# The gate of the down stage summed row by row in VectorE, its neighbour sum by accumulating DMAs, and values back in a new order

## The chip, the cores and the metric

The kernel runs on one core of a Trainium2 chip. The time is that of one execution on the device, in microseconds (us). Five engines matter: TensorE (PE, its weight loads PEld), VectorE (DVE), ScalarE (ACT), GpSimd (POOL) and SyncE (SP). Each takes its instructions in order and waits on semaphores for the others. SP, POOL and ACT also issue DMAs.

## The reference

One transformer block over 512 tokens of width 2048. An adaptive layer norm makes six rows of 2048 numbers from the condition `c`; attention and a short convolution stand in the middle; the part that matters here is the feed-forward end, with 5632 columns:

```python
sh_a, sc_a, g_a, sh_f, sc_f, g_f = jnp.split(jax.nn.silu(c) @ ada_w[l] + ada_b[l], 6, axis=-1)
...
x = x + g_a[:, None, :] * (jnp.concatenate([y_conv, y_attn], axis=-1) @ w_out[l])

h = modulate(rms_norm(x, norm_ffn[l]), sh_f, sc_f)
x = x + g_f[:, None, :] * ((jax.nn.silu(h @ ffn_w1[l]) * (h @ ffn_w3[l])) @ ffn_w2[l])
```

All is float32. `g_f`, the last sixth, is the gate of the down stage: silu(c) times 2048 rows of `ada_w`.

## The kernel before

Every weight is split into a high and a low half (`whi`, rounded by a cast in ACT, L905; `wlo`, the rest, by a subtraction in DVE, L910), so that products of halves give float32 accuracy. The order of the instructions on each engine is set by a scheduler that keeps to the order of the code where it can.

The last stages are these. **w_out** (to 895 us) multiplies the mixed values by `w_out`, adds them to x (L856 and after) and prepares the second norm. The **up stage** (917 to 1862 us) goes over 44 blocks u of 128 columns of `ffn_w1` and `ffn_w3`. For each, `blocks` loads four pieces of 512 KB on SP's queue (11 and 21, the upper and lower half of the rows of w1; 12 and 22, of w3), 128 partitions with eight pieces of 512 bytes each. The first two blocks (`PLAIN`) are multiplied plainly. Every later one takes a Strassen-like scheme of seven products in place of eight, with sums of the weight pieces:

- `sum5`: t = 11 + 12 into a tile of the pool `t2`; `sum6`: t += 22; `sum7`: 12 += 22; `sum4`: 21 += t. All four are DVE instructions of 128x1024, at L1006.
- The products p1, p5, p6, p3, p2, p7 and p4 multiply piece 11, t after sum5, t after sum6, 22, 21, the sum in 12 and the sum in 21 by the prepared inner values `hC[p]`. Each product is 16 matmuls (L917 with whi, L919 with wlo) into one of the PSUM banks x, y and z; p4 of a block is done two products into the next block (`late`).
- `post` evicts: ACT copies half a bank (L927), DVE adds the other (L928) or adds both (L924), ACT applies Silu, DVE multiplies (L1040), and `store` writes the 128 columns to the DRAM tensor `gd` on POOL's queue (L969).

A step of the main loop prepares the sums three products ahead (five for p4), the splits two ahead, and then issues its matmuls and its eviction. Raw pieces stand in `ring[0]` (4 buffers) and, for two blocks of three, in `raw2` (8 buffers, opened at step 7, when the memory of the second norm is free).

Beside this runs `gate_rows`, a generator of which the loop takes a step every third product. It computes `g_f` in four pieces of 512 columns. For each of 16 rows k of a piece it loads 128x512 of `ada_w` into the one buffer `raw` (L1107, 256 KB, POOL's queue), scales it in ACT by silu(c) (L1108) and adds it to `acc` in POOL (L1109). Both tiles are called `acc` in the profile and in the rows below. A matmul with ones sums over partitions, and a DMA keeps the result in `gfd`.

The **down stage** (1875 to 2281 us) multiplies by `ffn_w2` in the same manner, groups b of ten blocks. `k_load` reads five blocks of `gd` per half (L1164, POOL's queue), `a_parts` splits them (ghi in ACT at L1196, glo in DVE at L1197), `w_load` loads weights on SP and adds a second piece by an accumulating DMA of POOL's queue (L1208). `multiply` is L1248. A **tail** does the last four blocks and writes out 512 columns at a time.

## Time and profile before

| | us |
|---|---|
| median of 3 runs | 2335.28 |
| lowest, highest | 2333.3, 2337.05 |
| the profiled execution | 2334.18 |
| its span in the trace | 2332.4 |
| mean granted TensorE clock | 0.981 |

The span runs from the first to the last recorded instruction; 1.8 us of the execution lie around it. In a row of a group, the words behind the line and the engine are the operation, what it writes and reads by the program's names, the size in partitions x elements, and a count; in brackets at the end of a row of the timeline stands the idle time of the engine before the instruction and what ended it. In the rows of one source line three durations in ns follow (least, median, largest) and the first and last start. A row of the waits names the engine, tile and line that waited, whom it waited for, and the total, the times and the longest.

### The profile page before, as it was taken

The page shows a single profiled execution, that of the slowest core. Times are in us where ns is not written, and L with a number is a line of the kernel's source. Part 1 is how long each engine was busy: PE and PEld are TensorE (multiplying, and loading weights), DVE is VectorE, ACT ScalarE, POOL GpSimd, SP SyncE. Part 2 cuts the span into 40 slices and gives each one's busy share as a digit, 9 for nine tenths or more (in the row PEclk, how much of TensorE's full clock was granted, in tenths as well). Part 3 has the DMA queues.
Part 4 walks back from the last instruction along what each step waited for, and adds up shares of the span by engine and source line. Part 5 has one row for each costly group of instructions (what it writes and reads, how often), then busy time and mean ns, then how long its engine had stood idle before and what let it go on. Part 6 is the DMA issues. An engine that isn't in the chain of part 4 may idle for free. (4 is left out here: it accounts for less than half of the span.)

```text
span 2332.4 us, 30434 instructions
## 1 busy us (share of the span) xinstructions
PE 2205.1 (95%) x11401; PEld 1829.1 (78%) x11401; DVE 1795.3 (77%) x2555; ACT 1028.1 (44%) x1618; POOL 291.2 (12%) x381
## 2 busy tenths in 40 slices
PE   6999999999999997999989889899999889999998
PEld 5788788787787785788878778788888767787877
DVE  6868478878757745888778788788888767788888
ACT  5335245555542225444444444444444454444441
POOL 5400000000000012200320312300000021111001
PEclk9999999999999998999999999999999989999999
DMA  9964555544346853544444444444443388676645
GB/s 323 364 208 138 168 173 172 150 137 141 107 134 238 301 193 95 170 129 122 141 131 122 142 130 139 133 122 122 122 122 105 115 256 259 173 243 188 173 136 171
DMA packets 344928, 391.14 MB, mean 168 GB/s; under 512 B 16788, under 2 KB 257656, under 8 KB 343628
## 3 DMA queue, kind: packets, MB, share of 16 engines
q1 hardware_dynamic: 314556, 281.36, 38.3%
q0 software_dynamic: 30224, 107.84, 15.7%
q8 instruction: 89, 1.46, 0.2%
q14 instruction: 59, 0.48, 0.1%
HBM read 369.21 MB, written 19.93 MB: 167 GB/s over the span
## 5 line engine op out<-in xcount | busy, mean ns | idle before, releaser
L917 PE MATMUL main<-hC,whi 128*128 128x512 f32 x1408 | 369.7, 406 | 41.0 <-DVE d L924 21.2
L910 DVE TENSOR_TENSOR wlo<-raw,whi 128x1024 fp32r<-128x1024 f32 x218 | 270.5, 1241 | 113.5 <-ACT whi L905 112.9
L905 ACT CAST whi<-raw 128x1024 fp32r<-128x1024 f32 x238 | 248.7, 1045 | 210.5 <-PE main L917 99.3
L917 PEld LDWEIGHTS main<-hC,whi 128*128 128x128 f32 x1408 | 261.4, 195 | 95.9 <-DVE d L928 19.2
L917 PE MATMUL aux<-hC,whi 128*128 128x512 f32 x1072 | 272.1, 396 | 5.7 <-ACT whi L905 5.2
L905 ACT CAST whi<-t 128x1024 fp32r<-128x1024 f32 x144 | 151.1, 1051 | 194.1 <-PE aux L917 47.7
L917 PEld LDWEIGHTS aux<-hC,whi 128*128 128x128 f32 x1072 | 194.7, 191 | 43.7 <-ACT whi L905 6.7
L919 PEld LDWEIGHTS main<-hC,wlo 128*128 128x128 f32 x1408 | 195.8, 194 | 15.7 <-DVE wlo L910 1.4
L919 PE MATMUL main<-hC,wlo 128*128 128x256 f32 x1408 | 200.0, 286 | 0.0
L92 ACT CAST whi<-raw 128x1024 fp32r<-128x1024 f32 (+2 forms) x92 | 87.9, 958 | 214.3 <-PE main L100 137.0
L98 PE MATMUL main<-alo,whi 128*128 128x512 f32 x448 | 180.1, 402 | 1.4 <-DVE alo L346 1.4
L185 DVE SCALAR_TENSOR_TENSOR acc<-araw,cT,acc 128x512 f32<-128x512 f32 x184 | 137.8, 750 | 55.8 <-DMA araw<-in_ada_w 48.6
L99 PE MATMUL main<-ahi,wlo 128*128 128x512 f32 x448 | 176.8, 395 | 0.0
L100 PE MATMUL main<-ahi,whi 128*128 128x512 f32 x448 | 176.5, 394 | 0.0
L919 PEld LDWEIGHTS aux<-hC,wlo 128*128 128x128 f32 x1072 | 146.8, 191 | 12.7 <-DVE wlo L910 2.4
L93 DVE TENSOR_TENSOR wlo<-raw,whi 128x1024 fp32r<-128x1024 f32 (+2 forms) x92 | 102.0, 1113 | 68.1 <-ACT whi L92 67.3
L98 PE MATMUL main<-wlo,ahi 128*128 128x512 f32 x384 | 152.5, 397 | 1.1 <-DVE t L856 0.9
L919 PE MATMUL aux<-hC,wlo 128*128 128x256 f32 x1072 | 151.0, 284 | 0.8 <-DVE wlo L910 0.8
L99 PE MATMUL main<-whi,alo 128*128 128x512 f32 x384 | 150.4, 392 | 0.0
L100 PE MATMUL main<-whi,ahi 128*128 128x512 f32 x384 | 150.3, 391 | 0.0
L1248 PE MATMUL main<-wlo,ghi 128*128 128x512 f32 x280 | 110.7, 397 | 21.0 <-ACT ghi L1196 13.3
L910 DVE TENSOR_TENSOR wlo<-t,whi 128x1024 fp32r<-128x1024 f32 x84 | 104.4, 1243 | 25.3 <-ACT whi L905 25.3
(332 smaller groups left out, 4337.3 us busy)
## 6 DMA issues: line engine op xcount, KB each, us to landing
raw<-in_ffn_w SPq DMA_DIRECT2D x204, 512.0 KB, 4.0
w<-in_ffn_w SPq DMA_DIRECT2D x60, 512.0 KB, 5.9
araw<-in_ada_w POOLq DMA_DIRECT2D x56, 512.0 KB, 14.4
araw<-in_ada_w SPq DMA_DIRECT2D x112, 256.0 KB, 2.9
raw<-in_w_in SPq DMA_DIRECT2D x128, 192.0 KB, 2.7
araw<-in_ada_w SPq DMA_DIRECT2D x40, 512.0 KB, 5.5
raw<-in_w_in SPq DMA_DIRECT2D x37, 512.0 KB, 5.3
raw<-in_w_out SPq DMA_DIRECT2D x32, 512.0 KB, 5.8
```

Source lines behind the costliest of these rows:

```text
L92: nc.scalar.copy(hi[:, :m], raw[:, :m])
L93: nc.vector.tensor_sub(lo[:, :m], raw[:, :m], hi[:, :m].bitcast(F32))
L98: nc.tensor.matmul(ps, lhs[0], rhs[1], start=first, stop=False)
L99: nc.tensor.matmul(ps, lhs[1], rhs[0], start=False, stop=False)
L100: nc.tensor.matmul(ps, lhs[0], rhs[0], start=False, stop=last)
L185: nc.vector.scalar_tensor_tensor(acc, w, s, acc, op0=ALU.mult, op1=ALU.add)
L905: nc.scalar.copy(hi, t)
L910: nc.vector.tensor_sub(lo, t, hi.bitcast(F32))
L917: nc.tensor.matmul(ps, wt[0][:, ks[k]], hC[p][:, k, :], start=first and k == 0, stop=False, skip_group_check=True)
L919: nc.tensor.matmul(ps[:, HS:], wt[1][:, ks[k]], hC[p][:, k, 0:HS], start=False, stop=last and k == HK - 1, skip_group_check=True)
L1248: nc.tensor.matmul(ps[2 * t + c], x_[:, j, tok], w[:, cs], start=m == 0 and j == 0 and p in (1, 5, 2), stop=m == 2 and j == GC - 1 and p i ...
```

## The change

In `gate_rows` the ACT scale and the POOL add become one DVE instruction (raw times silu(c) plus acc), and the generator's `yield` stands between the DMA and this instruction. `sum5` is gone: from block 2 on, `blocks` loads piece 11 twice, the second time into the tile t, and POOL's queue issues an accumulating DMA that adds piece 12 to it. Odd blocks go to `raw2` and fill five of its buffers, even ones to `ring[0]` and `t2`. The pools `up` and `t2` stay open through the down stage. The tiles hC are allocated in another order; the last block's products come as p1, p5, p4 of the block before, p6, p3, p7, p2, p4. The post of the very last product is put behind the first `a_parts` of the down stage, and its store goes on ACT's queue. In the down stage the first splits of weights come ahead of the first `a_parts`, the calls of `a_parts` for p1 and p5 of a group and `k_load` come at other products, and the tail takes its columns in the order 2, 3, 0, 1.

```diff
--- before.py
+++ after.py
@@ -883,10 +883,10 @@
 
     HS, HK = S // 2, KC // 2
     ust = ExitStack()
+    dp = pool("up", 2)
+    t2p = pool("t2", 1)
     hcp = pool("hC", 1, stack=ust)
-    hC = {p: hcp.tile([P, HK, S], F32R, name=f"hC{p}") for p in (1, 2, 5, 6, 3, 7, 4)}
-    dp = pool("up", 2, stack=ust)
-    t2p = pool("t2", 1, stack=ust)
+    hC = {p: hcp.tile([P, HK, S], F32R, name=f"hC{p}") for p in (1, 5, 6, 3, 7, 2, 4)}
     PLAIN = 2
     NU = FF // P
     zone = {0: ring[0]}
@@ -894,10 +894,15 @@
     def blocks(u):
 
         b = {}
-        pl = zone[1] if u > PLAIN and u % 3 else ring[0]
-        for q, w, r0 in ((11, w1, 0), (21, w1, HK), (12, w3, 0), (22, w3, HK)):
-            b[q] = pl.tile([P, HK * P], F32, tag="raw", name="raw")
-            nc.sync.dma_start(b[q].rearrange("p (k n) -> p k n", k=HK), rows(w, r0, HK, u * P, P))
+        pl = zone[1] if u % 2 and 1 in zone else ring[0]
+        src = {q: rows(w, r0, HK, u * P, P) for q, w, r0 in ((11, w1, 0), (21, w1, HK), (12, w3, 0), (22, w3, HK))}
+        for name in (11, 21, 12, 22) if u < PLAIN else (11, "t", 21, 12, 22):
+            pl_, tag = (t2p, "t2") if name == "t" and pl is ring[0] else (pl, "raw")
+            b[name] = pl_.tile([P, HK * P], F32, tag=tag, name=tag)
+            to = b[name].rearrange("p (k n) -> p k n", k=HK)
+            nc.sync.dma_start(to, src[11 if name == "t" else name])
+        if u >= PLAIN:
+            nc.gpsimd.dma_start(b["t"].rearrange("p (k n) -> p k n", k=HK), src[12], accum_op=ALU.add)
         return b
 
     def w_hi(t):
@@ -966,7 +971,7 @@
             zone[1] = pool("raw2", 8, stack=ust, side="right")
 
     def store(f, g):
-        nc.gpsimd.dma_start(gd[f], g)
+        (nc.gpsimd if f + 1 < NU else nc.scalar).dma_start(gd[f], g)
 
     def plain_steps(u):
         o = {}
@@ -1004,10 +1009,6 @@
 
         def add(to, x, y):
             nc.vector.tensor_add(to, x, y)
-
-        def sum5():
-            o["b"]["t"] = t2p.tile([P, HK * P], F32, tag="t2", name="t2")
-            add(o["b"]["t"], o["b"][11], o["b"][12])
 
         def sum6():
             add(o["b"]["t"], o["b"]["t"], o["b"][22])
@@ -1051,12 +1052,17 @@
 
         none = lambda: None
         return [make(1, 11, none, "x", True, False),
-                make(5, "t", sum5, "y", True, False),
+                make(5, "t", none, "y", True, False),
                 make(6, "t", sum6, "x", False, False),
                 make(3, 22, none, "y", False, True),
                 make(2, 21, none, "z", True, True),
                 make(7, 12, sum7, "x", False, False),
                 make(4, 21, sum4, "x", False, True)]
+
+    def last_steps(new):
+
+        p1, p5, p6, p3, p2, p7, p4 = new
+        return [p1, p5], [p6, p3, p7, p2, p4]
 
 
     order, late = [], None
@@ -1070,10 +1076,11 @@
             late = None
         if u < PLAIN:
             order += new[2:]
+        elif u == NU - 1:
+            order += last_steps(new)[1]
         else:
             order += new[2:-1]
             late = new[-1]
-    order.append(late)
 
     begun = set()
 
@@ -1105,16 +1112,15 @@
             nc.gpsimd.dma_start(acc[0:1, :], a["ada_b"][:, c0:c0 + 512])
             for k in range(KC):
                 nc.gpsimd.dma_start(raw, ada_v[:, k, c0:c0 + 512])
-                nc.scalar.activation(raw, raw, AF.Identity, scale=cT[:, k:k + 1])
-                nc.gpsimd.tensor_add(acc, acc, raw)
                 yield
+                nc.vector.scalar_tensor_tensor(acc, raw, cT[:, k:k + 1], acc, op0=ALU.mult, op1=ALU.add)
             ps = aux()
             nc.tensor.matmul(ps[0:1, :], ones[:, 0:1], acc, start=True, stop=True)
             nc.scalar.copy(raw[0:1, :], ps[0:1, :])
             nc.gpsimd.dma_start(gfd[:, n * 512:(n + 1) * 512], raw[0:1, :])
 
     gate = gate_rows()
-    lead = {id(t): 5 if t["p"] == 4 and t is not order[-1] else 3 for t in order}
+    lead = {id(t): 3 if t["p"] != 4 else 2 if t is order[-1] else 5 for t in order}
     for n in range(3):
         prepare(n, "sum")
     for n in range(2):
@@ -1123,7 +1129,7 @@
     modulated(0, 2, 2, 3)
     modulated(0, 4, 4, 3)
     for n, s in enumerate(order):
-        for m in range(n + 5, n + 2, -1):
+        for m in range(n + 5, n + 1, -1):
             if m < len(order) and lead[id(order[m])] == m - n:
                 prepare(m, "sum")
         if n + 5 < len(order):
@@ -1134,7 +1140,8 @@
         if n >= 4 * PLAIN and n % 3 == 0:
             next(gate, None)
         s["mm"](s)
-        s["post"](s)
+        if n + 1 < len(order):
+            s["post"](s)
     ust.close()
 
 
@@ -1193,8 +1200,8 @@
                 src = {5: e, 6: e, 3: e, 7: a21, 2: a12, 4: a22}[p]
         hi = gpp.tile([P, GC, HS], F32R, tag="ghi", name="ghi")
         lo = gpp.tile([P, GC, HS], F32R, tag="glo", name="glo")
-        nc.scalar.copy(hi[:, :n], src)
-        nc.vector.tensor_sub(lo[:, :n], src, hi[:, :n].bitcast(F32))
+        A_["first"] = nc.scalar.copy(hi[:, :n], src).ins
+        A_["last"] = nc.vector.tensor_sub(lo[:, :n], src, hi[:, :n].bitcast(F32)).ins
         A_[b, p] = hi, lo
 
     def w_load(b, p, j):
@@ -1272,20 +1279,28 @@
     k_load(0, 1)
     for n in range(-10, 0):
         loads(n)
-    a_parts(*prods[0])
-    for m in range(3):
-        w_sum(*units[m])
     for m in range(2):
         w_split(*units[m])
+    a_parts(*prods[0])
+    with tc.issue_after(A_["last"]), tc.issue_after(A_["first"]):
+        order[-1]["post"](order[-1])
     a_parts(*prods[1])
     nc.sync.dma_start(gf, gfd.to_broadcast([P, D]))
     for n, (b, p, j) in enumerate(units):
         if j == 0:
-            a_parts(*prods[n // GC + 2])
-            if p == 3:
+            q = n // GC
+            if p == 1 and b:
+                a_parts(b, 5)
+            if p not in (2, 4):
+                a_parts(*prods[q + 2])
+            elif p == 2:
                 k_load(b + 1, 0)
-            elif p == 2 and b + 1 < NG:
-                k_load(b + 1, 1)
+            else:
+                if b + 1 < NG:
+                    k_load(b + 1, 1)
+                a_parts(*prods[q + 1])
+                if b + 1 == NG:
+                    a_parts(*prods[q + 2])
         loads(n)
         if n + 3 < len(units):
             w_sum(*units[n + 3])
@@ -1295,7 +1310,7 @@
         if j == GC - 1:
             evict(b, p)
 
-    for n in range(4):
+    for m, n in enumerate((2, 3, 0, 1)):
         cs = slice(n * 512, (n + 1) * 512)
         for i in range(NT):
             y = y2[:, i, cs]
@@ -1303,7 +1318,7 @@
             nc.gpsimd.dma_start(r, xd[n][:, i, :])
             nc.vector.tensor_mul(y, y, gf[:, cs])
             (nc.vector.tensor_add if n < 2 else nc.vector.tensor_sub)(y, r, y)
-        pst = [(aux if n % 2 else main)() for _ in range(NT)]
+        pst = [(aux if m % 2 else main)() for _ in range(NT)]
         ws = [load_split(ring, rows(w2, f, 2, n * 512, 512), 2, 512) for f in tail[::2]]
         for i in range(NT):
             tok = slice(i % 2 * P, (i % 2 + 1) * P)
```

How this moves instructions is shown at three places. First DVE within the up stage while gate rows run, at block 10; `d_...` are the tiles of the evictions, `t_...` the third sum. Before:

```order
L928 TENSOR_TENSOR d_9879<-main,d_9879 128x256
L910 TENSOR_TENSOR wlo<-raw,whi 128x1024
L1006 TENSOR_TENSOR t_9964<-raw 128x1024
L924 TENSOR_TENSOR d_9879<-aux,d_9879 128x256
L910 TENSOR_TENSOR wlo<-raw,whi 128x1024
L924 TENSOR_TENSOR d_9879<-aux,d_9879 128x256
L1006 TENSOR_TENSOR raw<-raw 128x1024
L924 TENSOR_TENSOR d_9855<-aux,d_9855 128x256
L910 TENSOR_TENSOR wlo<-t_9964,whi 128x1024
L924 TENSOR_TENSOR d_9855<-aux,d_9855 128x256
L1006 TENSOR_TENSOR t_9964<-t_9964,raw 128x1024
L924 TENSOR_TENSOR d_9879<-main,d_9879 128x256
```

And now, in the same block:

```order
L915 TENSOR_TENSOR wlo<-raw,whi 128x1024
L933 TENSOR_TENSOR d_9868<-aux,d_9868 128x256
L1116 SCALAR_TENSOR_TENSOR acc<-acc,cT 128x512
L915 TENSOR_TENSOR wlo<-raw,whi 128x1024
L933 TENSOR_TENSOR d_9655<-main,d_9655 128x256
L1011 TENSOR_TENSOR raw<-raw,t_9692 128x1024
L1041 SCALAR_TENSOR_TENSOR d_9687<-d_9687,d_9655 128x512
L933 TENSOR_TENSOR d_9868<-main,d_9868 128x256
L915 TENSOR_TENSOR wlo<-raw,whi 128x1024
L1116 SCALAR_TENSOR_TENSOR acc<-acc,cT 128x512
L929 TENSOR_TENSOR d_9868<-aux,d_9868 128x256
L915 TENSOR_TENSOR wlo<-raw,whi 128x1024
```

The write of t from two raw pieces is no longer there, and the gate's multiply-add (L1116) stands between splits and evictions.

ACT at the same block before, with the gate's scale between the casts and the evictions:

```order
L1027 ACTIVATE d_9855<-d_9855 128x256
L1108 ACTIVATE acc<-acc,cT 128x512
L905 CAST whi<-t_9964 128x1024
L927 COPY d_10037<-main 128x256
L905 CAST whi<-raw 128x1024
L1108 ACTIVATE acc<-acc,cT 128x512
L927 COPY d_10061<-aux 128x256
L905 CAST whi<-raw 128x1024
L927 COPY d_9855<-main 128x256
L1108 ACTIVATE acc<-acc,cT 128x512
L1039 ACTIVATE d_9855<-d_9855 128x256
```

And now, where the scale is gone and only casts, evictions and Silu are left:

```order
L910 CAST whi<-raw 128x1024
L932 COPY d_9868<-main 128x256
L910 CAST whi<-raw 128x1024 x3
L1028 ACTIVATE d_9844<-d_9844 128x256
L910 CAST whi<-raw 128x1024
L932 COPY d_10025<-main 128x256
L910 CAST whi<-raw 128x1024
L932 COPY d_10049<-aux 128x256
L910 CAST whi<-raw 128x1024
L932 COPY d_9844<-main 128x256
```

Second, POOL at blocks 8 to 10. Before, each gate DMA is followed by its add:

```order
L1109 TENSOR_TENSOR acc<-acc 128x512
L1107 DMA acc<-in_ada_w 128x512
L969 DMA gd_6507<-d_9879 128x512
L1109 TENSOR_TENSOR acc<-acc 128x512
L1107 DMA acc<-in_ada_w 128x512
L1109 TENSOR_TENSOR acc<-acc 128x512
L1107 DMA acc<-in_ada_w 128x512
```

Now (L905 is the accumulating DMA, L974 the store of a block):

```order
L974 DMA gd_6506<-d_9687 128x512
L1114 DMA acc<-in_ada_w 128x512
L905 DMA t_10054<-in_ffn_w 128x8x128
L1114 DMA acc<-in_ada_w 128x512 x2
L974 DMA gd_6507<-d_9868 128x512
L1114 DMA acc<-in_ada_w 128x512
L905 DMA raw<-in_ffn_w 128x8x128
```

The adds are gone, and accumulating DMAs stand among the gate's DMAs and the stores.

Third, POOL at the end of the up stage, with the last stores to `gd` (the last block's is gd_6540) and the first reads k of the down stage. Before:

```order
L969 DMA gd_6539<-d_15662 128x512
L1303 DMA r<-xd_6493 128x512 x2
L1164 DMA k_16002<-gd_6497 128x512
L1164 DMA k_16002<-gd_6498 128x512
L1164 DMA k_16002<-gd_6499 128x512
L1164 DMA k_16002<-gd_6500 128x512
L969 DMA gd_6540<-d_15838 128x512
L1164 DMA k_16002<-gd_6501 128x512
L1164 DMA k_16008<-gd_6502 128x512
```

Now:

```order
L974 DMA gd_6539<-d_15639 128x512
L1318 DMA r<-xd_6495 128x512 x2
L1171 DMA k_15973<-gd_6497 128x512
L1171 DMA k_15973<-gd_6498 128x512
L1171 DMA k_15973<-gd_6499 128x512
L1171 DMA k_15973<-gd_6500 128x512
L1171 DMA k_15973<-gd_6501 128x512
L1171 DMA k_15979<-gd_6502 128x512
L1171 DMA k_15979<-gd_6503 128x512
```

The store of the last block is no longer on this queue, and the reads of both halves of the first group follow each other.

## The prediction

> **What bounds the kernel now.** I read the page's busy times first, then windows over the up stage (917 to 1862 us), then that stage's waits, then the timeline inside one of its slow stretches.
>
> ```profile
> PE 2205.1 (95%) x11401; PEld 1829.1 (78%) x11401; DVE 1795.3 (77%) x2555; ACT 1028.1 (44%) x1618; POOL 291.2 (12%) x381
> 960.00:1040.00 80.00, 73.14 (x396) 63.07 (x395) 63.50 (x80) 34.06 (x49) 5.70 (x6) 0.96 0.55 158
> 1120.00:1520.00 400.00, 364.81 (x1965) 312.32 (x1964) 316.70 (x383) 188.29 (x278) 106.81 (x119) 0.96 0.45 135
> 1520.00:1600.00 80.00, 80.00 (x451) 69.45 (x450) 69.07 (x93) 36.92 (x53) 2.70 (x5) 0.99 0.41 123
> 1600.00:1840.00 240.00, 240.00 (x1376) 211.22 (x1375) 205.71 (x271) 111.38 (x160) 6.47 (x12) 1.00 0.36 110
> ```
>
> PE is the bound overall. A window row gives the stretch, its length, then busy time and instruction count of PE, PEld, DVE, ACT and POOL, granted clock, DMA share and GB/s. The last row holds no gate work (POOL 6.47 us): PE never idles and does 1376/240 = 5.73 matmuls a us at clock 1.00, with DVE busy 206/240 = 86%. The 400 us row holds gate rows (POOL 106.81): 1965 matmuls, which at 5.73 need 342.7 us. So 57.3 us are lost there; by the same division 10.9 us in 960 to 1040 and 1.3 us in 1520 to 1600, **69.5 us** in all.
>
> The waits of 1120 to 1520 and the timeline at 1305 us show how:
>
> ```profile
> POOL acc L1109 <- ACT acc L1108: 143.1, 45, 4.6
> ACT acc L1108 <- DMA acc<-in_ada_w: 110.9, 42, 5.1
> DVE wlo L910 <- ACT whi L905: 58.5, 42, 3.8
> PE main L917 <- DVE d L924: 19.2, 8, 3.3
> PE main L917 <- DVE d L928: 15.5, 11, 3.2
> 1283.36 1.82 DVE L1006 TENSOR_TENSOR t<-raw 128x1024 f32<-128x1024 f32 x1
> 1286.91 1.21 DVE L1006 TENSOR_TENSOR raw<-raw 128x1024 f32<-128x1024 f32 x1
> 1305.65 0.72 ACT L1108 ACTIVATE acc<-acc,cT 128x512 f32<-128x512 f32 x1 [4.15 <-DMA acc<-in_ada_w]
> 1307.52 0.36 ACT L927 COPY d<-main 128x256 f32<-128x256 f32 x1
> 1309.80 2.50 PE L917 MATMUL main<-hC,whi 128*128 128x512 f32 x5 [3.15 <-DVE d L928]
> ```
>
> ACT is only 44% busy, but takes its instructions in order. The row's scaling (L1108) stands in that queue until its DMA lands, 111/42 = 2.6 us a time; the eviction L927 and the casts L905 stand behind it, DVE waits for the casts, and PE waits for the eviction because its bank is not free. POOL's adds are a second, smaller harm: L1006 took 1.82 us beside one and 1.21 without.
>
> **The change, part by part.**
>
> *Gate rows.* Sixty-four times an ACT scale and a POOL add go, and a DVE multiply-add comes. The trace has each, and the new one's twin at L185, with the same shape:
>
> ```profile
> L1108 ACT ACTIVATE acc<-acc,cT x64: 716/724/730, 858.5 to 1513.4; 128x512 f32<-128x512 f32 x64
> L1109 POOL TENSOR_TENSOR acc<-acc x64: 1255/1287/2970, 859.3 to 1514.2; 128x512 f32<-128x512 f32 x64
> L1107 POOL DMA_DIRECT2D acc<-in_ada_w x64: 546/553/582, 853.4 to 1510.7; - x64
> DMA to landing us min/median/max: 2.7/3.0/5.1
> L185 DVE SCALAR_TENSOR_TENSOR acc<-araw,cT,acc x184: 735/752/754, 298.2 to 834.4; 128x512 f32<-128x512 f32 x184
> L1006 DVE TENSOR_TENSOR t<-raw x42: 1208/1220/2325, 961.1 to 1830.0; 128x1024 f32<-128x1024 f32 x42
> ```
>
> DVE gets 64 x 0.752 = 48.1 us and loses the third sums, 42 x 1.22 = 51.2 us, so in total it is no busier. While the gate runs it is: a block of 128 columns takes 19.5 us (112 matmuls at 5.73), DVE now works 0.86 x 19.5 = 16.7 us in it, less 1.22, plus about 2.5 gate rows (the new DVE order) x 0.752 = 1.9, so 17.4 us or 89%. PE ran without a gap at 86%, so this should nearly hide. What is new is that the in-order wait for the row's DMA now stands on DVE. The next DMA goes out behind the multiply-add (one buffer): about 0.3 us of semaphore, then 3.0 us (5.1 at worst) to landing, 3.3 in all. Between two gate rows DVE has some 5 us of other work or more (in the piece of its new order shown above, six instructions: three of 1.2, one of 0.7 and two of 0.4 us). So a row has mostly landed. I charge 4 us of PE time for the late ones; the bounds are 0 and, if DVE waited as ACT did (2.6 us for each of the 54 rows in the up stage), all that the gate costs now. I take the near end, since the median of 3.0 is the nearest row.
>
> *First Strassen blocks.* Of the 10.9 us in 960 to 1040, the larger part is no gate loss:
>
> ```profile
> 980.00:1000.00 20.00, 15.45 (x71) 12.99 (x70) 11.35 (x15) 5.30 (x9) 0.00 (x0) 0.83 0.89 252
> 990.83 1.23 DVE L1006 TENSOR_TENSOR t<-raw 128x1024 f32<-128x1024 f32 x1 [7.02 <-DMA raw<-in_ffn_w]
> ```
>
> 71 matmuls instead of 20 x 5.73 = 115 is 7.6 us, and DVE waits there for a load of block 3, which shares the four buffers of block 2. After, block 3 is odd and loads all its five pieces into the second pool as soon as that opens. I take 6 of the 7.6 back (bounds 0 and 7.6; the loads of three blocks still collide there).
>
> *Accumulating DMAs.* 42 of them replace the sums. They are not in the up stage's trace, but the down stage has forty of the same 512 KB, in long pieces:
>
> ```profile
> L1208 POOL DMA_DIRECT2D t<-in_ffn_w x20: 848/857/941, 1871.5 to 2185.0; - x20
> DMA to landing us min/median/max: 5.1/8.8/21.2
> q1 hardware_dynamic: 50566, 25.49, 36.2%
> q1 hardware_dynamic: 10364, 35.85, 37.7%
> q0 software_dynamic: 5751, 20.20, 35.3%
> t<-in_ffn_w POOLq DMA_DIRECT2D x15, 512.0 KB, 9.5
> k<-gd POOLq DMA_DIRECT2D x25, 256.0 KB, 4.1
> w<-in_ffn_w POOLq DMA_DIRECT2D x11, 512.0 KB, 8.2
> ```
>
> The first two rows are of the whole run; the first q1 row (packets, MB, share of 16 engines) is of 1560 to 1800 us, the rest of 1940 to 2200. Up stage: 36.2% of 240 us for 25.49 MB is 1.79 us of all 16 engines for 512 KB, which go in 512-byte pieces (27.5 ns a packet on its engine). Down stage: a plain 512 KB costs 0.377 x 260 x 0.524/35.85 = 1.43 us; of q0's 0.353 x 260 = 91.8 us, 25 reads of 256 KB at that price take 17.9, which leaves 73.9/26 = 2.84 us for an accumulate, **twice a plain load**. So I take 3.6 us in the up stage, an estimate from these rows. With store and gate row (0.5 and at most 1.9 us, sized by their bytes and the two plain prices) a block then needs 5 x 1.79 + 3.6 + 2.4 = 15 of its 19.5 us: it hides. Bounds: 1.8 us (a plain load), and, if the price went by packet and not by byte, 13 us; that end is the slower rival. Issuing them costs POOL 42 x 0.86 = 36 us, where 64 x 1.29 of adds go.
>
> The Trainium skill, "DMA: Bandwidth & Descriptors", section "Why small descriptors are slow (HBM only)", puts the penalty of small pieces at about three bus cycles and 32 bytes each, which would make 512-byte pieces a fifth or so dearer by the byte. The trace agrees for plain loads (1.79 against 1.43 us); no run here shows it for accumulates. By it the sum would not change.
>
> *Ramp from w_out.* DVE's first L910 waits behind ACT's scales:
>
> ```profile
> 898.76 1.46 DVE L910 TENSOR_TENSOR wlo<-raw,whi 128x1024 fp32r<-128x1024 f32 x1 [9.18 <-ACT whi L905]
> ```
>
> With them gone the w_out residual starts earlier: 1.5 us (0 to 3).
>
> *Hand-over to the down stage.*
>
> ```profile
> 1850.14 2.12 POOL L1164 DMA_DIRECT2D k<-gd  x4
> 1857.87 2.55 PE L917 MATMUL main<-hC,whi 128*128 128x512 f32 x8 [2.08 <-DVE d L924]
> 1865.24 0.54 POOL L969 DMA_DIRECT2D gd<-d  x1 [12.98 <-DVE d L1040]
> 1868.87 2.64 POOL L1164 DMA_DIRECT2D k<-gd  x5 [2.56 <-issue]
> 1874.09 1.26 ACT L1196 CAST ghi<-k 128x1280 fp32r<-128x1280 f32 x1 [9.87 <-DMA k<-gd]
> 1875.40 1.65 PE L1248 MATMUL main<-wlo,ghi 128*128 128x512 f32 x3 [13.28 <-ACT ghi L1196]
> 1875.40:1895.00 19.60, 19.36 (x74) 15.16 (x75) 14.17 (x11) 9.22 (x11) 1.71 (x2) 0.89 1.05 308
> 1895.00:2281.00 386.00, 371.32 (x1609) 303.13 (x1608) 320.82 (x322) 178.59 (x174) 49.89 (x71) 0.99 0.66 193
> ```
>
> PE waits 2.08 us before its last product (same bank as the one before) and 13.28 us after it, because the fifth gate-and-up read (k) stands behind the last store, which waits 12.98 us for the last post. After, the store is on ACT's queue, all five reads go out near 1853 to 1856, land by 1860 (median 4.1 us in the down stage's DMA row), the cast ends near 1861. PE then waits about 2.5 us for it and runs some 2 us slow. The gap before was 2.1 + 13.3 us, and some 3.8 of low clock (the last product took 1.3 us more than its like, and 74 matmuls after the restart 19.6 us where 1609/371.32 = 4.33 a us gives 17.1): 19 us. I take 12 of it back; bounds 6 (if the first accumulates, now issued behind ten reads, come late) and 16.
>
> *Down stage and tail.* PE idles 14.7 of 386 us (last row). The reads and parts are moved by a product or two, but the waits for accumulates stay. I take 0.5 us, bounds -4 and +5.
>
> **Sum:** gate 61.9 - 4 = 58, first blocks 6, ramp 1.5, hand-over 12, rest 0.5: 78 us off the profiled run's 2334.18 gives 2256.2. The median shown is 1.1 us above that run, so **2257 us**.
>
> **Rivals.**
>
> That ACT keeps the rows is ruled out by the order above. What is left:
>
> *B: DVE becomes the gate's victim.* It is in order, and wlo and evictions stand behind a multiply-add whose row isn't there. It decides once a row lands later than some 4.7 us after its issue (5 less the semaphore). For it: the landing's maximum of 5.1, and five loads a block on the same engines. Against: the median 3.0, and 11% spare on DVE. If half of the gate's cost stays, 2257 + 58/2 + a few = about **2290**.
>
> *C, slower: accumulates of 512-byte pieces bound the up stage.* If the extra is per packet, as large as in the down stage's 4 KB pieces (1.41 us x 16/128 = 176 ns on an engine), one takes 64 x (27.5 + 176) = 13 us, and a block on average 9 + 13 + 1.5 = 23.5 against 19.5: 42 x 4 = 168 us on top of the forecast, about **2425**. It begins to bind above 9 us for one accumulate and eats the whole gain above 11. For: no row shows accumulates of small pieces. Against: plain loads in pieces eight times shorter cost only 1.79/1.43 = 1.25 times as much by the byte.
>
> *D: accumulates land late for p5 though there is room.* In even blocks about 20 us lie between issue and use (seven products of 2.8 us); beyond that PE waits. Landing was 8.8 at the median, 21.2 at most. Late by 3 us in 21 even blocks takes 63 us back: about **2320**; by 4, no gain.
>
> The skill, "SBUF — State Buffer", section "Who interferes with whom", says that POOL can be starved of the port for writing descriptors by some DVE operations, though not by tensor_tensor, and advises other queues. By that rule an 89% busy DVE would push D. Here L1107's issue stays between 546 and 582 ns among DVE's work, so this trace shows no such starving; the sum by the rule would be D's.
>
> **How the numbers follow.** Forecast 0.68 (own range 2242 to 2272), B 0.15, C 0.10, D 0.07. The range from 2242 to 2300 holds most of the first two. Faster by over 0.2% (what a measurement of this kernel can tell from no change): 0.68 + 0.15 + 0.04 of D = 0.87; within: 0.02 of D; slower: C and 0.01 of D, 0.11.
>
> **What would show it.** Right: windows of 80 us in 1120 to 1520 near 455 matmuls, DVE near 90% busy in gate phases, few waits of DVE for in_ada_w, the restart of the down stage some 3 us after the last up product. B: DVE waits for in_ada_w of 1 us and more each, and PE behind wlo. C: DMA share near 1 through the up stage. D: PE waiting before p5 of even blocks alone. The forecast fails most easily in the accumulate's price, which is carried over from long pieces to short ones.

## The result and the profile after

| | before | changed |
|---|---|---|
| median of 4 runs, us | 2334.29 | 2300.27 |
| lowest, highest | 2331.09, 2337.05 | 2297.38, 2305.64 |
| span of the profiled execution | 2332.4 | 2295.6 |

The ratio is 0.9857, with a 95% interval from 0.9835 to 0.9880: 34 us or 1.4% faster. The forecast was 2257 us, 77 us faster, with a range up to 2300. The direction came out, the size didn't: less than half of the gain is there, and the time lies just outside the range.

Where the two traces part, by stage (first and last matmul of each stage, in us):

| | before | changed | difference |
|---|---|---|---|
| start to the last product of w_out | 895.1 | 901.9 | +6.8 |
| to the first product of the up stage | 22.4 | 18.5 | -3.9 |
| up stage | 944.6 | 902.7 | -41.9 |
| to the first product of the down stage | 13.3 | 7.2 | -6.1 |
| down stage | 405.1 | 413.1 | +8.0 |
| tail | 51.9 | 52.2 | +0.3 |

The first row isn't the change's: 6 us of it arise between 740 and 820 us (312 matmuls against 339), where all engines have the same order in both kernels, and a second trace of the kernel before, below, has 905.1 there. So the 36.8 us between the traces are 42 in the up stage and 4 in the ramp, less the 7 of the first row and the 2 by which the down stage gives back more than the hand-over's 6.

The busy line of the changed kernel's page:

```profile
PE 2197.4 (96%) x11401; PEld 1822.9 (79%) x11401; DVE 1758.1 (77%) x2577; ACT 989.5 (43%) x1554; POOL 263.9 (11%) x358
```

PE has 8 us less of busy time and 37 us less of span, DVE 37 us less work, POOL 27. Its windows, with the columns of those before:

```profile
960.00:1040.00 80.00, 74.27 (x407) 64.63 (x406) 57.82 (x77) 33.06 (x46) 10.09 (x9) 0.96 0.90 211
1120.00:1520.00 400.00, 386.97 (x2174) 335.21 (x2173) 329.95 (x453) 176.32 (x255) 70.37 (x92) 1.00 0.77 196
1600.00:1760.00 160.00, 160.00 (x917) 140.74 (x916) 128.15 (x172) 73.49 (x105) 18.72 (x17) 1.00 0.73 176
```

The last row has accumulations but no gate rows, and loses no matmul. The 400 us with gate rows now have 2174 matmuls in place of 1965: at 5.73 a us they lose 20.6 us where they lost 57.3. The 80 us from 960 lose 9.0 us where they lost 10.9. The DMA share is 0.77 where it was 0.45. DVE's waits for DMAs in the 400 us (total, times, longest):

```profile
DVE raw L1011 <- DMA raw<-in_ffn_w: 31.8, 8, 5.2
DVE acc L1116 <- DMA acc<-in_ada_w: 27.3, 11, 6.5
```

The rows of three source lines, L1116, L1114 (the gate rows' DMA, its landing) and L905 (the accumulation, issue and landing):

```profile
L1116 DVE SCALAR_TENSOR_TENSOR acc<-acc,cT x64: 735/746/755, 865.1 to 1511.3; 128x512 f32<-128x512 f32 x64
DMA to landing us min/median/max: 2.6/4.2/8.6
L905 POOL DMA_DIRECT2D t<-in_ffn_w x21: 1545/1577/1618, 909.6 to 1757.6; - x21
DMA to landing us min/median/max: 6.2/8.3/11.6
```

The gate's instruction costs the 0.75 us that were expected. Gate rows land in 4.2 us, in 3.0 before. ACT's wait for rows is gone, but DVE now stands 59 us before two kinds of DMA: the seventh product's sum of even blocks (L1011) for its load, and the gate's instruction for its row. The evictions stand behind both. Of PE's 14 gaps of over 0.15 us in the 400 (12.9 us together), 12 (11.4 us) come when the sum's wait was the last that DVE had, as at 1204 us below. The gate instruction's waits take up the time that DVE has to spare before that; how much of PE's loss this makes is not shown here.

```profile
1204.04 1.23 DVE L1011 TENSOR_TENSOR raw<-raw 128x1024 f32<-128x1024 f32 x1 [5.24 <-DMA raw<-in_ffn_w]
1205.18 0.42 DVE L933 TENSOR_TENSOR d<-aux,d 128x256 f32<-128x256 f32 x1
1205.66 3.44 PE L922 MATMUL aux<-hC,whi 128*128 128x512 f32 x8 [2.53 <-DVE d L933]
...
1217.81 1.60 POOL L905 DMA_DIRECT2D raw<-in_ffn_w  x1 [4.25 <-issue]
1221.35 0.57 POOL L1114 DMA_DIRECT2D acc<-in_ada_w  x1 [1.94 <-DVE acc L1116]
1227.81 0.75 DVE L1116 SCALAR_TENSOR_TENSOR acc<-acc,cT 128x512 f32<-128x512 f32 x1 [3.82 <-DMA acc<-in_ada_w]
```

The row issued at 1221.35, while the accumulation of 1217.81 is under way, is used 6.5 us later, where L1107 landed in 3.0 before. PE has no gap behind this wait.

### The profile page after: what moved, and what is told of

Read it like the earlier page. It is cut to its first block, busy times and chain, and to the rows that moved or that the text cites. A ratio compares the mean times of both kernels' runs of the same rounds, so it can differ in the third digit from the quotient of the medians.

```text
span 2295.6 us, 30548 instructions
## 1 busy us (share of the span) xinstructions
PE 2197.4 (96%) x11401; PEld 1822.9 (79%) x11401; DVE 1758.1 (77%) x2577; ACT 989.5 (43%) x1554; POOL 263.9 (11%) x358
## 5 line engine op out<-in xcount | busy, mean ns | idle before, releaser
L910 ACT CAST whi<-raw 128x1024 fp32r<-128x1024 f32 x280 | 292.8, 1048 | 306.7 <-PE main L922 132.3
L922 PE MATMUL main<-hC,whi 128*128 128x512 f32 x1408 | 356.9, 395 | 9.2 <-DVE d L933 5.2
L915 DVE TENSOR_TENSOR wlo<-raw,whi 128x1024 fp32r<-128x1024 f32 x260 | 315.6, 1217 | 47.2 <-ACT whi L910 45.7
L922 PEld LDWEIGHTS main<-hC,whi 128*128 128x128 f32 x1408 | 253.6, 189 | 60.0 <-DVE d L933 7.3
L922 PEld LDWEIGHTS aux<-hC,whi 128*128 128x128 f32 x1072 | 195.4, 191 | 51.9 <-DVE d L933 14.8
L910 ACT CAST whi<-t 128x1024 fp32r<-128x1024 f32 x102 | 107.2, 1052 | 126.5 <-PE main L1255 32.3
L1011 DVE TENSOR_TENSOR raw<-raw 128x1024 f32<-128x1024 f32 x84 | 102.3, 1218 | 59.7 <-DMA raw<-in_ffn_w 59.5
```

What stands on the lines that cost most here:

```text
L910: nc.scalar.copy(hi, t)
L915: nc.vector.tensor_sub(lo, t, hi.bitcast(F32))
L922: nc.tensor.matmul(ps, wt[0][:, ks[k]], hC[p][:, k, :], start=first and k == 0, stop=False, skip_group_check=True)
L1011: nc.vector.tensor_add(to, x, y)
```

## The experiments

Each ratio is to the kernel before on the same chip (the chips' own medians for it go from 2334 to 2344 us), with its 95% interval. "Up" is the up stage in the run's trace, "matmuls" those of 1120 to 1520 us, where a stage without loss has 2279. Where intervals overlap, the order of two runs is not shown.

| run | ratio | up, us | matmuls |
|---|---|---|---|
| before | 1 | 944.6 | 1965 |
| the change | 0.9857 (0.9835 to 0.9880) | 902.7 | 2174 |
| after_again | 0.9857 (0.9824 to 0.9890) | 907.6 | 2137 |
| before_again | one run, 2345.51 us | 941.1 | 1986 |
| acc_only | 1.0083 (1.0062 to 1.0103) | 956.4 | 1910 |
| gate_only | 0.9695 (0.9678 to 0.9713) | 874.1 | 2279 |
| par_sum5 | 0.9702 (0.9681 to 0.9722) | 874.0 | 2279 |
| plain_t | 0.9733 (0.9702 to 0.9763) | 877.2 | 2279 |
| sum5_extra | 0.9693 (0.9668 to 0.9718) | 875.0 | 2272 |
| odd_acc | 0.9758 (0.9733 to 0.9783) | 888.2 | 2206 |
| last21 | 0.9864 (0.9843 to 0.9884) | 919.3 | 2079 |
| after7 | 0.9854 (0.9832 to 0.9875) | 907.0 | 2104 |
| gate2 | 0.9811 (0.9783 to 0.9840) | 896.1 | 2197 |
| after7_gate2 | 0.9763 (0.9734 to 0.9793) | 891.6 | 2191 |
| row_sp | 0.9794 (0.9773 to 0.9815) | 896.9 | 2192 |
| row_sp2 | 0.9766 (0.9745 to 0.9786) | 892.6 | 2219 |
| old_loop | 0.9837 (0.9816 to 0.9858) | 909.7 | 2129 |
| sum5_old_hand | 0.9722 (0.9686 to 0.9757) | 878.5 | 2279 |
| sum5_gate2 | 0.9675 (0.9640 to 0.9709) | 874.7 | 2279 |

**The two halves apart.** acc_only puts the old gate back, gate_only the old loads and the sum in DVE.

```diff
 # acc_only
-                nc.vector.scalar_tensor_tensor(acc, raw, cT[:, k:k + 1], acc, op0=ALU.mult, op1=ALU.add)
+                nc.scalar.activation(raw, raw, AF.Identity, scale=cT[:, k:k + 1])
+                nc.gpsimd.tensor_add(acc, acc, raw)
 # gate_only: blocks() as before, and
-                make(5, "t", none, "y", True, False),
+                make(5, "t", sum5, "y", True, False),
```

> The changed kernel with the gate rows as before (ACT scales, POOL adds); the accumulating DMAs and everything else of the change stay. Theory G (the gain of the up stage comes from taking the row's wait off ACT): the up stage goes from about 904 us back towards 945, time 2330 to 2345, with ACT again waiting some 110 us for in_ada_w. Rival L (the gain comes from the loads: third sum by DMA, new pools): the up stage stays under 915, time under 2312.

> The changed kernel with the four loads and the third sum in DVE as before; the gate rows in DVE stay. Theory Q (what is left of the gate's loss, about 21 us in 1120 to 1520, is DVE standing in order behind waits for DMAs that the extra DMA traffic made later): with DMA share back near 0.5 the gate rows land in about 3 us again instead of 4.2, the waits of the gate's instruction fall from 57 us to under 20, and though DVE has 1.2 us more per block the up stage takes 895 to 905: time 2290 to 2303. Rival B (DVE's own work is the bound in the gate phases): 1.2 us more per block makes it worse, up stage 912 or more, time 2308 or more.

acc_only is slower than the kernel before, beyond what theory G had. Its ACT waits for rows in 1120 to 1520:

```profile
ACT acc L1115 <- DMA acc<-in_ada_w: 138.0, 44, 6.0
```

That is 3.1 us a time, where it was 2.6 in the waits of before. So the accumulating loads cost something with the rows in ACT too. gate_only is 38 us faster than the change would be on its chip (0.9857 - 0.9695 = 0.0162 of 2344), and the window and then DVE's wait for rows show why:

```profile
1120.00:1520.00 400.00, 400.00 (x2279) 349.24 (x2278) 372.08 (x497) 185.45 (x267) 40.34 (x75) 1.00 0.51 152
```

```profile
DVE acc L1115 <- DMA acc<-in_ada_w: 1.5, 1, 1.5
```

PE never idles, though DVE is 372/400 = 93% busy. So moving the gate is all of the gain, and more than the change keeps; the accumulating loads are a loss. Theory Q came out beyond its range (874 instead of 895 to 905), rival B fell.

**The rule for the pools, or the load itself.** par_sum5 keeps the new rule (even blocks in the ring) and takes only the fifth load and the accumulation out; plain_t leaves all issues where they are but drops the accumulation.

```diff
 # par_sum5 (and sum5 for the fifth product, as in gate_only)
-        for name in (11, 21, 12, 22) if u < PLAIN else (11, "t", 21, 12, 22):
+        for name in (11, 21, 12, 22):
...
-            nc.gpsimd.dma_start(b["t"].rearrange("p (k n) -> p k n", k=HK), src[12], accum_op=ALU.add)
 # plain_t
-            nc.gpsimd.dma_start(b["t"].rearrange("p (k n) -> p k n", k=HK), src[12], accum_op=ALU.add)
+            nc.gpsimd.dma_start(b["t"].rearrange("p (k n) -> p k n", k=HK), src[12])
```

> The changed kernel without fifth load and accumulating DMA (third sum in DVE as before), but with the new rule for the pools: even blocks in the four buffers of the ring, odd ones in raw2. Known so far: the change runs at 0.986 of before, with old loads and old pool rule at 0.970. Theory R (the rule costs: in even blocks the seventh product's sum stands on DVE and waits for piece 22, whose buffer comes free last): the waits of the sums for in_ffn_w stay near 2 to 3 us for each even block and the ratio is 0.980 to 0.986. Theory A (the fifth load and the accumulation cost, by DMA time or by their place on POOL's queue): 0.968 to 0.974, and these waits nearly vanish.

> The changed kernel with the accumulating DMA as a plain DMA on the same queue (t then holds piece 12 alone, so the result is another): same issues and waits, but half of the DMA engines' time for it. Theory A1 (the DMA engines' time of the accumulation makes every load late): DMA share falls from 0.78 to about 0.65 in gate phases, gate rows land nearer to 3.4 us, ratio 0.974 to 0.980. Theory A2 (the place on POOL's queue costs, where stores and gate rows stand behind accumulations that wait for t's first load): ratio 0.983 to 0.988, as the change.

The rule costs nothing that can be seen. The fifth load with a plain DMA in the accumulation's place costs 0.003, and the intervals overlap; with the accumulation it is 0.0155. The window of plain_t and, apart, its waits:

```profile
1120.00:1520.00 400.00, 400.00 (x2279) 349.38 (x2278) 348.56 (x475) 186.07 (x267) 58.59 (x94) 1.00 0.68 206
```

```profile
DVE raw L1011 <- DMA raw<-in_ffn_w: 12.0, 10, 2.2
DVE acc L1116 <- DMA acc<-in_ada_w: 8.8, 10, 2.1
```

DVE waits 21 us instead of 59, and PE loses nothing. Theory A2 fell and theory A1 is a little exceeded: the accumulation itself costs, not the place alone. Gate rows issued while the plain DMA was under way landed in 4.0 us at the median (12 rows), the others in 3.9. In the change it is 5.4 us under an accumulation (14 rows) and 3.8 for the rest.

**Is it the DMA engines' time?** sum5_extra adds three plain loads per block that nobody reads to par_sum5. odd_acc accumulates in odd blocks alone, whose t is loaded far ahead.

```diff
 # sum5_extra, behind each load but the last of a block
+                with tc.issue_after(ld):
+                    nc.sync.dma_start(extra.rearrange("p (k n) -> p k n", k=7), rows(w3, 0, 7, u * P, P))
 # odd_acc (and sum5 in even blocks)
-        for name in (11, 21, 12, 22) if u < PLAIN else (11, "t", 21, 12, 22):
+        for name in (11, "t", 21, 12, 22) if u > PLAIN and u % 2 else (11, 21, 12, 22):
```

> The version with the third sum in DVE (par_sum5, ratio 0.970) plus three plain loads of 448 KB per block on SP's queue into a tile that nobody reads: some 4.8 us of DMA engines' time per block, so that their share rises from 0.50 to about 0.75 in gate phases, near the 0.77 of the change. Theory E (the engines' time alone costs, by making gate rows and loads land late): gate rows land in 4.3 us or more, DVE waits for them and for loads, ratio 0.976 to 0.984. Rival (plain traffic is harmless; it needs the accumulation, by its own lateness or its place on POOL's queue): 0.970 to 0.973.

> The changed kernel with the fifth load and the accumulating DMA in odd blocks alone; even blocks sum in DVE as before. Theory E: half of the extra engine time, DMA share near 0.64, ratio 0.974 to 0.979. Rival T (t comes late in even blocks only): 0.970 to 0.973. Rival B (the cost is of odd blocks, whose accumulations stand in POOL's queue ahead of gate rows): 0.980 to 0.986.

> The changed kernel itself on the chip of the other two, for direct comparison: ratio 0.984 to 0.988, up stage 900 to 912 us.

Here theory E, mine by then, fell. Two windows of sum5_extra and, apart, its loads' issues (count, KB, us to landing; on SP's queue the trace gives the landing of about a third of the DMAs):

```profile
960.00:1040.00 80.00, 80.00 (x459) 70.33 (x458) 70.70 (x92) 36.19 (x53) 2.17 (x4) 1.00 0.89 261
1120.00:1520.00 400.00, 399.27 (x2272) 348.38 (x2272) 367.89 (x492) 184.89 (x267) 39.25 (x73) 1.00 0.72 219
```

```profile
raw<-in_ffn_w SPq DMA_DIRECT2D x81, 512.0 KB, 4.0
```

With 219 GB/s, more than the change's 196, and nearly its DMA share, the loads land in 4.0 us (5.4 in the change) and only 7 matmuls are lost. In 960 to 1040 the share is the change's (0.89 against 0.90), and it does 459 matmuls where the change does 407. odd_acc loses about half (14 of the 29 us of the up stage), so lateness in even blocks alone isn't it either; its ratio lies in theory E's range too. Its timeline shows the place again: an accumulation on POOL's queue, a gate row issued while it is under way, and DVE.

```profile
1203.12 1.59 POOL L905 DMA_DIRECT2D raw<-in_ffn_w  x1 [5.45 <-DMA raw<-in_ffn_w]
1206.93 0.56 POOL L1120 DMA_DIRECT2D acc<-in_ada_w  x1 [2.22 <-DVE acc L1122]
1213.76 0.75 DVE L1122 SCALAR_TENSOR_TENSOR acc<-acc,cT 128x512 f32<-128x512 f32 x1 [5.66 <-DMA acc<-in_ada_w]
```

The row takes 6.8 us to its use. In the 120 us from here, DVE waited at most 0.8 us for a row that followed no accumulation, the first row of a piece aside.

**The rows off that queue.** row_sp sends them on SP's queue, row_sp2 also gives them two buffers, gate2 has two buffers on POOL's queue.

```diff
 # row_sp
-                nc.gpsimd.dma_start(raw, ada_v[:, k, c0:c0 + 512])
+                nc.sync.dma_start(raw, ada_v[:, k, c0:c0 + 512])
 # gate2 (row_sp2 the same with nc.sync), raws = the old buffer and a new one
+                if k + 1 < KC:
+                    nc.gpsimd.dma_start(raws[(k + 1) % 2], ada_v[:, k + 1, c0:c0 + 512])
+                raw = raws[k % 2]
```

> The changed kernel with two buffers for gate rows, the next row's DMA issued one row ahead. Theory G2 (the gate instruction's in-order waits for its row, 57 us in all, are what is left): these waits fall below 15 us, in the up stage and at the end of the stage before it, ratio 0.976 to 0.982. Rival S (the sums' waits for their loads alone decide): gate waits fall but the ratio stays 0.983 to 0.987.

> The changed kernel with accumulations as they are, but the gate rows' DMAs on SP's queue, with two buffers (gate2, the same with the rows on POOL's queue, gave 0.981). Theory F (a row's DMA, or a store's, issued behind an accumulation on POOL's queue lands only when that is through: 6.5 to 6.8 us instead of 3): rows land in under 4.2 us at the median and none waits behind an accumulation, waits of the gate's instruction in 1120 to 1520 fall from gate2's 22 us to under 8, ratio 0.974 to 0.978. Rival (any DMA is slowed while an accumulation runs, whatever its queue): rows land in 4.3 us or more, ratio 0.980 to 0.983.

> The same with one buffer, as in the changed kernel (0.986): SP then holds loads back while a row waits for its buffer. Theory F: waits of the gate's instruction fall below 15 us in 1120 to 1520, ratio 0.977 to 0.982, less than with two buffers since loads come late. Rival: 0.984 to 0.990.

gate2 takes 12 us of the 57 of waits for rows in the whole run, not 42, and its ratio lies in theory G2's range. In row_sp, with every accumulation still there, the recorded landings are like those of the kernel before; behind that row stand the waits of 1120 to 1520:

```profile
DMA to landing us min/median/max: 2.5/3.0/5.0
```

```profile
DVE raw L1011 <- DMA raw<-in_ffn_w: 31.9, 9, 4.5
DVE acc L1116 <- DMA acc<-in_ada_w: 26.3, 11, 6.4
```

The two don't fit each other. The trace gives the landing of only 20 of row_sp's 64 rows, and in 1120 to 1520 none of these was issued while an accumulation was under way. Those that were, 14 there as in the change, can be followed to their use. DVE waited for 7 of them and used them 4.9 to 6.2 us after their issue on SP's queue (median 5.5). In the change, on POOL's queue, it waited for 7 as well, and used them after 4.7 to 6.6 us (median 5.5). One of row_sp's; the accumulation of the first line lands at 1212.7:

```profile
1206.18 1.56 POOL L905 DMA_DIRECT2D raw<-in_ffn_w  x1 [4.59 <-issue]
1210.06 0.60 SPq L1114 DMA_DIRECT2D acc<-in_ada_w  x1
1216.14 0.75 DVE L1116 SCALAR_TENSOR_TENSOR acc<-acc,cT 128x512 f32<-128x512 f32 x1 [3.17 <-DMA acc<-in_ada_w]
```

So the runs don't show that the order within POOL's queue makes these rows late. Theory F's ratios came in both runs, but its waits did not: 26 us with one buffer, as in the change, and 17.5 with two (14 for rows, the rest for the bias) where it had under 8. Its landing in row_sp2, 3.8 us, is that of 21 rows in 63; in 1120 to 1520 the 8 of them issued under an accumulation took 4.9 us at the median, 7 others 3.3. That is the rival's mechanism (any DMA is slowed while an accumulation runs), though the rival's ratios didn't come. Nor is this clean: each of the 7 rows of row_sp stood 1.0 us behind a weight load on SP's own queue, and rows 0.6 us behind such a load, without an accumulation, landed in 3.7 to 5.0 us. Why both versions are faster than the change is not shown.

The sums' wait stays in both (31.9 and 28.6 us), and here too an accumulation is under way. In the change all eight loads for which the sum waits in 1120 to 1520 were issued on SP's queue during one, and used 5.5 to 7.7 us after their issue. In gate_only the loads whose landing is known took 3.9 us at the median and 5.3 at most.

**The sums' wait.** last21 loads piece 21 last, after7 keeps the seventh product's sum behind the split of the second product and prepares it two products ahead; after7_gate2 is after7 with two row buffers.

```diff
 # last21
-        for name in (11, 21, 12, 22) if u < PLAIN else (11, "t", 21, 12, 22):
+        for name in (11, 21, 12, 22) if u < PLAIN else (11, "t", 12, 22, 21):
 # after7, Z["lo"] being the last split in DVE
-            add(o["b"][12], o["b"][12], o["b"][22])
+            with tc.issue_after(Z["lo"]):
+                add(o["b"][12], o["b"][12], o["b"][22])
```

> The changed kernel with the five loads of a block in the order 11, t, 12, 22, 21 in place of 11, t, 21, 12, 22, so that pieces 12 and 22 no longer queue behind the buffer of 21, which the late p4 frees last. Theory S (the seventh product's sum in even blocks waits for these loads, 59.5 us over 21 times, and in gate phases this wait is what PE loses): that wait falls below 15 us and the up stage by 8 to 15 us, time 2285 to 2293. Rival: DVE has slack where it waits, or the wait moves to piece 21: up stage within 3 us of 904, time 2297 to 2304.

> The changed kernel with the seventh product's sum kept behind the split of the second product, two products ahead of its use instead of up to six, so that DVE no longer meets it before piece 22 has landed. Theory S (this wait on DVE, 59.5 us in the up stage, is what PE loses in the gate phases together with the gate rows' waits): waits of sums for in_ffn_w under 10 us, up stage 8 to 18 us shorter, ratio 0.978 to 0.982. Rival: DVE stands elsewhere instead (gate rows, later loads): ratio 0.984 to 0.988.

> The changed kernel with both waits of DVE softened: the seventh product's sum late (after7, alone 0.985) and two buffers for gate rows (gate2, alone 0.981). Theory W (the accumulation's engine time makes loads and rows land late, and PE loses only because DVE, in order, waits for them; each of the two edits alone moves the wait to the other place): together ratio 0.972 to 0.977, PE without gaps in 1120 to 1520. Rival (something else of the accumulation holds PE back, so the edits add nothing to each other): 0.980 to 0.983.

last21 missed: the sum still meets piece 22 too early (68.6 us in the whole stage instead of 59.5). after7 took that wait away altogether, and the time stayed, since DVE then reached the rows sooner and stood there, and ACT's casts, for which PE waits, came late:

```profile
DVE acc L1118 <- DMA acc<-in_ada_w: 61.8, 17, 5.7
PE main L923 <- ACT whi L911: 21.0, 13, 3.2
```

With both softened the ratio is 0.9763, as theory W had it, but PE still does 88 matmuls less than 2279 in the 400 us: PE waits 12.0 us for ACT's casts. This fits W in that each wait hides the other, but it doesn't show that nothing else is lost.

**The hand-over.** old_loop puts the down stage's loop back, sum5_old_hand is par_sum5 with the old hand-over, before_again is the kernel before.

```diff
 # old_loop
-            q = n // GC
-            if p == 1 and b:
-                a_parts(b, 5)
...
+            a_parts(*prods[n // GC + 2])
+            if p == 3:
                 k_load(b + 1, 0)
 # sum5_old_hand
-        if n + 1 < len(order):
-            s["post"](s)
+        s["post"](s)
...
-        (nc.gpsimd if f + 1 < NU else nc.scalar).dma_start(gd[f], g)
+        nc.gpsimd.dma_start(gd[f], g)
```

> The changed kernel with the down stage's main loop as before (parts two products ahead, gate-and-up reads at products 3 and 2); its beginning and the tail stay changed. Theory D (the new places of parts and reads make the down stage 8 us longer): down stage 405 instead of 413, time 2290 to 2294. Rival N (the 8 us are how DMAs happen to land, or come from the hand-over): down stage 409 to 417, time 2297 to 2305.

> The kernel before, unchanged, for its trace beside the next ones on the same chip. Theory H (the hand-over gains nothing: the restart is 6 to 12 us sooner but the first accumulations of the down stage come at the same time, so p5 waits instead): from the last product of the up stage to the last of the down stage it takes 417 to 424 us here too, as in all runs with the new hand-over (418 to 428). Rival: 425 to 432 here, that is, the new hand-over saves 6 us or more and only the first chip's traces hid it.

> The changed kernel with the third sum in DVE (par_sum5, ratio 0.970), and the hand-over as before: last products in the old order, last post and its store inside the up stage and on POOL's queue, parts of the first product ahead of the weight splits. Theory H: ratio 0.969 to 0.973, and from the last up product to the last down product 417 to 424 us. Rival (the new hand-over saves what it was predicted to, 6 to 12 us): ratio 0.973 to 0.976.

From the last up product to the last down product it takes 418.4 us before, 421.0 in before_again and 423.1 in sum5_old_hand, against 420.3 in the change, 425.8 in after_again, 424.9 in old_loop and 419.7 in par_sum5, whose PE restarts after 1.5 us instead of 13.3. In the other runs with the new hand-over it is 418 to 429. The new loop and the new hand-over save nothing that can be seen in the traces. The times decide less: sum5_old_hand's interval and par_sum5's overlap, and their difference of 0.002 (5 us) could be nothing or the 12 us that were forecast. Two windows of par_sum5 behind its restart suggest where the time goes:

```profile
1790.00:1810.00 20.00, 14.74 (x61) 11.29 (x62) 12.57 (x11) 7.04 (x8) 3.48 (x4) 1.00 1.01 322
1810.00:1830.00 20.00, 16.02 (x65) 11.58 (x65) 14.67 (x13) 12.47 (x16) 1.71 (x2) 1.00 1.05 316
```

The DMA engines are full (share 1.01 and 1.05) with weights and reads of the first group, and PE idles 9 of 40 us. In the change the casts wait 9.0 us for `t` there (2.1, once, in the 90 us behind the last up product of the kernel before):

```profile
ACT whi L910 <- DMA t<-in_ffn_w: 9.0, 4, 4.8
```

**A version that beats both.** sum5_gate2 is par_sum5 with gate2's second row buffer.

> The version that should beat both: the changed kernel with the third sum in DVE as before (par_sum5) and two buffers for gate rows. Nothing is left to gain in the up stage (par_sum5 loses no matmul there); what may go is the gate rows' wait ahead of the up stage, where the way from the last w_out product to the first up product was 15 us with two buffers and 19 to 21 with one: ratio 0.967 to 0.969. Rival: the rows' waits there are hidden by the second norm, ratio 0.970 to 0.971.

It took 2262.68 us where the kernel before took 2342.39: 0.9675, so it beats the kernel before by 3.3% and the change by 1.8%. Against par_sum5 the intervals overlap. In its trace, as in the others with two row buffers, the way from w_out to the up stage is 14 to 15 us instead of the change's 18.5.

## Why the prediction missed

- **The bound and the mechanism before were right.** The up stage lost its 57.3 us to rows that stood in ACT's queue. Without accumulations the moved gate takes the stage from 944.6 to 874.0 us, 70.6 less. The terms for this, 58 for the gate and 6 for the first Strassen blocks, were 7 too small: DVE hides the rows though it is 93% busy (it waited 1.5 us for them in 400, and I had charged 4), and the first blocks came back whole.
- **The step that failed is the accumulation, "it hides".** Its rows were read well: 3.6 us of the engines were estimated, and the trace gives 3.8 (q0's 25.3% of 200 us in 1560 to 1760 are 50.6 us; 10 stores at the plain price take 9.2; 41.4/11). It lands in 8.3 us, where I had 8.8 from the down stage. (The store was sized at 0.5 us, where 256 KB are 0.9 by my own plain price; the 15 of 19.5 us hold all the same.) But this sum looks at room on the engines and at the accumulation's own user alone. With the fifth load it costs 0.0155 of the time, 36 us, through others: gate rows issued while it is under way take 5.4 us to land instead of 3.8, and the loads on SP's queue 5.4 instead of 3.9 in gate_only. DVE then stands 59 us before them, where it stood 21 with a plain DMA in its place. This reaches PE only while gate rows run: the 160 us without rows lose nothing. It isn't bound to rows in DVE, since acc_only, with the rows in ACT, is slower than the kernel before.
- **Rival B was half of the mechanism, with too small a chance.** I had it at 0.15 and about 2290. Its point of decision, a row later than 4.7 us, is passed by rows issued under an accumulation (6.5 and 6.8 us to their use), and DVE waits 2.5 us each for 11 rows. But 31.8 of its 59 us are the sum's wait for a load on SP's queue, which B doesn't have, and most of PE's gaps follow that one. I took the rows' landing from the trace before, 3.0, though the change brings a second kind of DMA beside them. C and D didn't happen: the DMA share is 0.77, and the accumulations land in 11.6 us at most.
- **The first blocks** gave 2 us of the 6 in the change: their window still loses 9.0. The term's reason was wrong too. gate_only keeps the old rule, by which block 3 shares the four buffers of block 2, and loses nothing in the same window (458 matmuls), as par_sum5 with the new rule does (460). As far as the runs tell, the 10.9 us lost there before go with the gate rows in ACT, against my "no gate loss". The kernel before has this among its waits of 960 to 1040:

```profile
ACT acc L1108 <- DMA acc<-in_ada_w: 10.5, 2, 6.0
```

- **The ramp** gave 3.9 in these two traces where 1.5 was forecast; with one row buffer on POOL's queue and the gate in DVE it is 18.5 to 20.8 us in all runs, against 22.4 and 23.3 in the two traces of the kernel before.
- **The hand-over, 12 us, gave nothing that the traces show.** The reads land earlier and PE restarts sooner (after 7.2 us in the change and 1.5 in par_sum5, where some 3 were forecast). The next limit seems to be the first group's weights on full DMA engines; that is argued from the windows above, and no run tests it. I had named late accumulations as a bound of the range, at 6 us, and not worked out what the engines carry there.
- **Not settled:** how an accumulation makes other DMAs late, and how much of the loss is the rows' and how much the loads'. In acc_only the 8 rows issued under an accumulation in 1120 to 1520 landed in 3.4 us at the median, hardly later than the others (3.2). The rows on SP's queue give back 0.006, with two buffers 0.009 of the 0.0155, for a reason that no run shows.

The Trainium skill, "DMA: Bandwidth & Descriptors", section "Queues, rings and completion order", says that an engine takes descriptors of one queue in order and goes round between queues. No run here shows the order within a queue apart: with an accumulation under way on POOL's queue, a row was used 6.5 us after its issue on the same queue and 6.1 us after its issue on SP's.

## What to carry to other kernels

A DMA that fits into the engines' free time and lands in time for its own user can still cost: look at what else is under way with it, on its own queue and on others, and at which in-order engine waits for that. When a wait moves from one engine to another, take its length from the traffic of the new kernel, not of the old, and try the parts of a change apart: here one half was worth 70 us and the other cost half of that. Follow a late transfer from its issue to its use before a median of landings is believed: here the trace gave the landing of a third of the rows, and not of the late ones. When a stall at a stage's border is taken away, work out what the DMA engines must still bring for the products behind it.

## What was not expected of the hardware

An accumulating DMA of 512 KB in 512-byte pieces took 1.58 us to issue on POOL, against 0.86 in long pieces, and 0.90 for a plain one with the same pieces (plain_t). While such DMAs ran, plain loads on another queue landed in 5.4 us at a DMA share of 0.77; with plain traffic alone it was 4.0 at 0.72 (sum5_extra) and 4.6 at 0.68 (plain_t). And VectorE at 93% busy, in order, held up no matmul in the 400 us of gate_only.
